# One ScalarE table behind the last head, and later places for the first unit's heads

## The chip, the cores and the metric

The kernel runs on one core of a Trainium2 chip. The core has a matrix engine (TensorE, "PE" in the profile), a vector engine (VectorE, "DVE"), an engine for functions of single elements (ScalarE, "ACT"), a general one (GpSimd, "POOL") and one that issues transfers (SyncE, "SP"); 16 DMA engines move the data. Each engine works through its own instructions in their order and waits for others by semaphores. The metric is the device time of one execution in microseconds. The time before is the median of three runs, 1692.59 us (1690.44 to 1696.43).

## What is computed

One layer of a decoder trunk (DEPTH is 1, so the convolution layer of the reference is not run), for 256 rows of 4096 numbers, all in float32:

```python
def rms_norm(x, g):
    y = x * lax.rsqrt(jnp.mean(x * x, axis=-1, keepdims=True) + 1e-6)
    return y * g

def attn_branch(xn, w_in, w_out):              # w_in 4096 x 16384, w_out 4096 x 4096
    q, k, v, g = jnp.split(xn @ w_in, 4, axis=-1)
    o = stick_breaking_attention(heads(q), heads(k), heads(v))   # 32 heads of 128
    return (o * jax.nn.silu(g)) @ w_out

# stick-breaking, strictly causal (s < t), z = q k^T / sqrt(128):
#   log_a = log_sigmoid(z) + sum of log_sigmoid(-z) over the places between s and t
#   a = exp(log_a);  out = a @ v

h = x + attn_branch(rms_norm(x, norm_attn), w_in, w_out)
return rms_norm(h, final_norm)
```

## The kernel before

**The products.** The projection by w_in is cut into 16 units (0 to 15), each with 256 columns of q, k, v and gate, which are two heads. The projection by w_out follows as four units (16 to 19). A unit runs over 16 steps s of 256 rows of the weights. All products are made in float32 precision from two rounded parts: a value is cast into a high part ("wh" of a weight, "sh" or "oh" of the activations), and the low part is the difference ("wl", "sl", "ol"). Each product is then three matmuls of 512 columns, high by high, high by low and low by high. Most units replace the eight block products of a step by seven or eight of sums and differences of blocks, and so the weights themselves need sums as well (rows that write and read "raw").

**The flow of a weight.** SyncE loads a tile into one of seven buffers "raw"; GpSimd adds a block to some of them by a transfer that accumulates; ScalarE casts wh; VectorE subtracts for wl, which frees the raw buffer for the next load; TensorE multiplies into one of seven banks of PSUM ("acc"). A weight is called by its number below: wh36 and wl36 belong to part 36.

**The heads.** When a unit's q, k, v and gate stand in SBUF ("qk_sb", "gv_sb"), `gate` applies the SiLU on ScalarE, and `heads` runs two heads one behind the other, between the next unit's products. A head (`head`) goes to and fro: TensorE turns q and k ("tr"), ScalarE copies them ("qkT"), TensorE makes the scores ("z"), ScalarE makes the softplus ("f") and its high part ("fh"), VectorE the low part ("fl"), TensorE sums along the row with a triangle of -1 ("scan", z again), ScalarE takes the exponential ("a"), TensorE multiplies by v ("o"), and VectorE multiplies by the gate. One bank "att" is shared by all of this, so a head's steps wait for each other. What the heads give is spilled to DRAM and comes back as "p" for the second projection.

**The end.** `plain_h` copies unit 16's four banks into the output rows "h" on ScalarE, once the heads' last result is spilled; unit 17 writes the same banks again. Sums with x ("xres"), squares and the gain ("grow") follow unit by unit. For the last unit, `last_h`, `block_done`, `part_done` and `finish` end the two blocks of 128 rows (t = 1 first, then t = 0): last sums out of the banks, squares, then in `finish` the inverse root as exponential of -0.5 times a logarithm on ScalarE, one step of Newton on VectorE, and `rows_out` scales the block and stores its eight tiles.

**What sets the order.** The program is written by a planner (`Plan`): it holds a model of the engines' times, and whenever an engine is free in that model, it emits the waiting piece of work with the lowest key. A key is a place on TensorE's line of products in ns; `soon(c)` is the present place plus c us, and `act` without a key takes `soon()`, that is 4 us. So a number in a key moves instructions in one engine's order, and what moves there moves the model for all others.

**Tables.** ScalarE holds one set of functions at a time. The program loads one at its start, and a later pass puts a load ahead of each function that the present set lacks (rows ACT_TABLE_LOAD).

Of the kernel before, what the change touches and what calls it, by code (L numbers as in the profile page):

```python
# [13 lines left out]
AF = mybir.ActivationFunctionType  # L14
# [5 lines left out]
P = 128  # L20
S = 256
# [26 lines left out]
TABLE = 1400  # L48
# [17 lines left out]
H_LATER = 3  # L66
GAIN_LATER = 30.0
ON_SCALAR = ((1, 3, 5), (1, 3))
AHEAD, SUMS_AHEAD = 4.0, 4.0
BLOCKS_LATER = 2  # L70
FORMS_BEHIND = 3
# [34 lines left out]
def scalar_ns(n):  # L106
    return 98 + n / 1.2
# [142 lines left out]
def kernel(  # L250
# [10 lines left out]
    nc = Plan(tc)  # L261
# [14 lines left out]
    def minus(out_, full, part):  # L276
        nc.vector.tensor_tensor(out=out_, in0=full, in1=part.bitcast(F32), op=ALU.subtract)
# [49 lines left out]
    def soon(c=4.0):  # L327
        return nc.here + 1e3 * c


    def dve(emit, n, key=None, more=0, **kw):
        n = n if isinstance(n, tuple) else (n,)
        cost = sum(vector_ns(m) for m in n) + 122 * (len(n) - 1) + more
        return nc.work("vector", cost, emit, soon() if key is None else key, **kw)

    def act(emit, n, key=None, **kw):
        n = n if isinstance(n, tuple) else (n,)
        cost = sum(scalar_ns(m) for m in n) + 100 * (len(n) - 1)
        return nc.work("scalar", cost, emit, soon() if key is None else key, **kw)
# [6 lines left out]
    def ten(emit, *n, what):  # L346
        def others():
            nonlocal since_others, words
            first_ = BEHIND.get(what, ())
            since_others, words = 0, first_ + BEHIND_OTHERS[len(first_) :]  # L350
            emit()

        return nc.work("tensor", 40 + sum(tensor_ns(m) for m in n), others, nc.here - 1e4, wait=400)
# [453 lines left out]
    st, ev = {}, {}  # L807

    def gate(u):
        yield nc.until(("gv", u))  # L810
        g = st["gv", u][:, :, 0:CW]
        n = NT * CW
        yield act(lambda: nc.scalar.activation(g, g, AF.Silu), n + TABLE)
        nc.tell(("gate", u))

    def mm3(out_, a, b, start, stop, orders):
# [8 lines left out]
    BW = 3 * P  # L825
    not_before = off.broadcast_to([P, 2, P])

    def head(u, i):
        yield nc.take("att", "gh", sooner=True)
        tr = att.tile([P, 2, S], F32, tag="att", name=f"tr{u}_{i}")  # L830

        def turn():
            for k in range(2):
                for t in range(NT):
                    c = k * CW + i * P
                    nc.tensor.transpose(tr[:, k, t * P : (t + 1) * P], st["qk", u][:, t, c : c + P], ident)

        yield ten(turn, P, P, P, P, what=("turn", i))
        if i == HG - 1:
            nc.give("one")  # L840
        qk = wp.tile([P, 2, S], F32, tag="gh", name=f"qkT{u}_{i}", bufs=ROWS)
        yield act(lambda: nc.scalar.copy(qk, tr), 2 * S)
        nc.give("att")
        yield nc.take("att", sooner=True)
        bank = att.tile([P, W], F32, tag="att", name=f"z{u}_{i}")
        z, gT = bank[:, 0:BW], bank[:, BW:W]

        def turned(to, t):
            nc.tensor.transpose(to, st["gv", u][:, t, i * P : (i + 1) * P], ident)

        def scores():
            kw = dict(stop=False, skip_group_check=True)
            nc.tensor.matmul(z[:, 0:P], qk[:, 1, P:S], qk[:, 0, P:S], start=True, **kw)
            nc.tensor.matmul(z[:, P:BW], qk[:, 1, 0:P], qk[:, 0, :], start=False, **kw)
            diagonal = z[:, 0 : 2 * P].rearrange("p (a b) -> p a b", a=2)
            nc.tensor.matmul(diagonal, ident_b, not_before, start=False, **kw)

        yield ten(scores, *FULL_P, *FULL_S, 2 * P, what=("scores", i))
        nc.give("gh")
        yield nc.take("gh", sooner=True)  # L860

        f = wp.tile([P, BW], F32, tag="gh", name=f"f{u}_{i}", bufs=ROWS)

        def soft():
            nc.scalar.activation(f, z, AF.Softplus, scale=scale)
            nc.scalar.activation(f, f, AF.Copy, scale=1.0 / scale)

        yield act(soft, (BW + TABLE, BW))
        yield nc.take("gh", "gh", sooner=True)
        fh, fl = (wp.tile([P, BW], F32R, tag="gh", name=f"f{k}{u}_{i}", bufs=ROWS) for k in "hl")  # L870
        yield act(lambda: nc.scalar.copy(fh, f), BW)
        yield dve(lambda: minus(fl, f, fh), BW)
        nc.give("gh")

        if i == 0:
            yield nc.until(("gate", u))

        def scan():
            kw = dict(start=False, skip_group_check=True)
            nc.tensor.matmul(z, neg_tri, fh, stop=False, **kw)  # L880
            nc.tensor.matmul(z, neg_tri, fl, stop=False, **kw)
            nc.tensor.matmul(z[:, 2 * P : BW], neg_one, fh[:, 0:P], stop=False, **kw)
            nc.tensor.matmul(z[:, 2 * P : BW], neg_one, fl[:, 0:P], stop=True, **kw)
            turned(gT, 0)

        yield ten(scan, BW, BW, P, P, P, what=("scan", i))
        nc.give("gh", "gh")
        gated = st["gv", u][:, :, i * P : (i + 1) * P]
        yield nc.take("gh", sooner=True)
        a = wp.tile([P, BW], F32, tag="gh", name=f"a{u}_{i}", bufs=ROWS)  # L890


        def weights_of():
            nc.scalar.activation(a, z, AF.Relu, scale=-scale)
            nc.scalar.activation(a, a, AF.Exp, scale=-1.0)

        yield act(weights_of, (BW, BW + TABLE))
        yield act(lambda: nc.scalar.copy(gated[:, 0, :], gT), P)
        nc.give("att")
        yield nc.take("att", sooner=True)  # L900
        bank2 = att.tile([P, BW], F32, tag="att", name=f"o{u}_{i}")
        o, gT2 = bank2[:, 0:S], bank2[:, S:BW]
        v = lambda t: st["gv", u][:, t, CW + i * P : CW + (i + 1) * P]

        def out_of_head():
            kw = dict(skip_group_check=True)
            nc.tensor.matmul(o, v(0), a[:, P:BW], start=True, stop=False, **kw)
            nc.tensor.matmul(o[:, P:S], v(1), a[:, 0:P], start=False, stop=True, **kw)
            turned(gT2, 1)

        yield ten(out_of_head, *FULL_P, *FULL_S, P, what=("values", i))
        nc.give("gh")
        yield act(lambda: nc.scalar.copy(gated[:, 1, :], gT2), P)
        o2 = o.rearrange("p (t b) -> p t b", t=NT)
        yield dve(lambda: nc.vector.tensor_tensor(out=gated, in0=o2, in1=gated, op=ALU.mult), S)
        nc.give("att")
# [66 lines left out]
    def make_room():  # L983
        nonlocal ep
        rooms.close()
        ep = ctx.enter_context(tc.tile_pool(name="last", bufs=1))

    def new_h(c):

        if 2 <= c < NJ - 4:  # L990
            pair = wp.tile([P, KT, W], F32, tag="wh", name=f"h{c}", bufs=HIGHS)
            for t in range(NT):
                hs[c, t] = pair[:, t, :]
            return
        if c == NJ - 4:
            raw_h = raws[:, raw_free.pop(0)]
            for t in range(NT):
                hs[c, t] = raw_h[:, t].rearrange("p k n -> p (k n)")
            return
        for t in range(NT):  # L1000
            pool, tag, bufs = (ep, f"h{c}_{t}", 1)
            if c == NJ - 3 and t == 0:
                pool, tag, bufs = wp, "gh", ROWS
            elif c >= NJ - 2:
                pool, tag = sp, "x" + "hl"[t] + str(LAST_STEPS[c - NJ + 2])
            hs[c, t] = pool.tile([P, W], F32, tag=tag, name=f"h{c}_{t}", bufs=bufs)
# [67 lines left out]

    def plain_h(u, c):
        yield nc.until(*(("spilled", v) for v in range(NB)), ("full", u, PLAIN["C11"]))
        make_room()
        for k in range(2):
            new_h(c + k)
        for k in range(2):  # L1080
            for t in range(NT):
                b = PLAIN[f"C{t + 1}{k + 1}"]
                yield nc.until(("full", u, b))
                yield act(lambda: nc.scalar.copy(hs[c + k, t], ev[u][b]), W, place_of[u + 1, 0] - 2e3)
                nc.give(f"b{b}")
        nc.tell(("C", u))
# [121 lines left out]
    def rows_out(c, t, f, key):  # L1208
        h = hs[c, t]
        if c >= NJ - 2:  # L1210
# [6 lines left out]
            )  # L1217
        elif c in ON_SCALAR[t]:
            yield act(lambda: nc.scalar.activation(h, h, AF.Copy, scale=f), W, key)
# [75 lines left out]
    for s in range(NS):  # L1295
        nc.start(blocks_of_heads(s))
    U = OUT0
    nc.start(plain_h(U, 0))
    for k, c in enumerate(range(0, NJ - 2, 2)):
        if k:  # L1300
# [44 lines left out]
```

## Time and profile before

| | us |
|---|---|
| median of three runs | 1692.59 |
| profiled execution | 1690.6 |
| its span, first to last instruction | 1688.9 |
| ScalarE busy in table loads, 84 of 1283 ns and one at the start | 109.1 |
| TensorE waits: for VectorE's wl, 5 times | 3.6 |
| TensorE waits: for ScalarE's wh, once | 0.4 |
| last matmul ends | 1671.6 |

The profile is one execution. A row of the timeline shows start and length in us, the engine, the line of the program, the operation, the tile written and the tile read, the shape, and behind it in brackets how long the engine idled before it and for whom. Nearly all instructions have line 133, a helper's; tiles tell them apart. The granted clock of TensorE was 0.996 of full speed.

### The profile page before, as it was taken

The page shows a single profiled execution, that of the slowest core. Times are in us where ns is not written, and L with a number is a line of the kernel's source. Part 1 is how long each engine was busy: PE and PEld are TensorE (multiplying, and loading weights), DVE is VectorE, ACT ScalarE, POOL GpSimd, SP SyncE. Part 2 cuts the span into 40 slices and gives each one's busy share as a digit, 9 for nine tenths or more (in the row PEclk, how much of TensorE's full clock was granted, in tenths as well). Part 3 has the DMA queues.
Part 4 walks back from the last instruction along what each step waited for, and adds up shares of the span by engine and source line. Part 5 has one row for each costly group of instructions (what it writes and reads, how often), then busy time and mean ns, then how long its engine had stood idle before and what let it go on. Part 6 is the DMA issues. An engine that isn't in the chain of part 4 may idle for free.

```text
span 1688.9 us, 24974 instructions
## 1 busy us (share of the span) xinstructions
PE 1666.1 (99%) x7731; PEld 1409.2 (83%) x7731; DVE 1611.2 (95%) x1851; ACT 1268.8 (75%) x1668; POOL 365.8 (22%) x448
## 2 busy tenths in 40 slices
PE   9999999999999999999999999999999999999995
PEld 7888888888888888888888888888888888888884
DVE  8889999999999999999999999999999978999996
ACT  8886968686868696868686868787878766656665
POOL 0022222222222222222222222222222112212110
PEclk9999999999999999999999999999999999999998
DMA  9968898988897979797979798889888977979894
GB/s 338 349 177 252 230 261 222 259 227 257 228 265 212 274 202 281 199 285 206 272 215 265 215 260 227 247 235 251 231 249 239 291 247 239 274 223 275 249 307 148
DMA packets 253174, 417.22 MB, mean 247 GB/s; under 512 B 28784, under 2 KB 77168, under 8 KB 253040
## 3 DMA queue, kind: packets, MB, share of 16 engines
q1 hardware_dynamic: 194544, 354.24, 62.9%
q0 software_dynamic: 58208, 61.11, 21.9%
q8 instruction: 60, 0.98, 0.2%
q14 instruction: 74, 0.61, 0.1%
q10 hardware_dynamic: 288, 0.28, 0.1%
HBM read 407.13 MB, written 8.39 MB: 246 GB/s over the span
## 4 chain that ended last, share of the span: by engine, by line
PE 93%; DVE 4%; issue 1%; ACT 1%; DMA 1%; SPq 0%; DVEq 0%; ACTq 0%
PE acc L133 88%; PE z L133 3%; DVE wl L133 2%; PE o L133 1%; PE tr L133 1%; DVE h L133 1%; DVE raw L133 1%; DMA raw<-in_w_out_dram 0%; ACT wh L133 0%; DMA xres<-in_x_dram 0%; ACT L133 0%; DMA raw<-in_w_in_dram 0%; DVE wh L133 0%; SPq L133 0%; ACT sq L133 0%
## 5 line engine op out<-in xcount | busy, mean ns | idle before, releaser
L133 ACT CAST wh<-raw 128x1024 fp32r<-128x1024 f32 (+1 forms) x1019 | 936.5, 966 | 326.0 <-PE acc L133 139.3
L133 DVE TENSOR_TENSOR wl<-raw,wh 128x1024 fp32r<-128x1024 f32 (+1 forms) x830 | 989.8, 1219 | 42.8 <-ACT wh L133 19.5
L133 PE MATMUL acc<-wh,sh 128*128 128x512 f32 x2048 | 766.0, 387 | 0.4 <-ACT wh L133 0.4
L133 PE MATMUL acc<-wh,sl 128*128 128x512 f32 x1883 | 721.3, 383 | 0.0
L133 PE MATMUL acc<-wl,sh 128*128 128x512 f32 x1718 | 657.7, 383 | 2.2 <-DVE wl L133 2.2
L133 POOL DMA_DIRECT2D raw<-in_w_in_dram x330 | 284.0, 945 | 1003.5 <-DMA raw<-in_w_in_dram 409.6
L133 PEld LDWEIGHTS acc<-wh,sh 128*128 128x128 f32 x2048 | 384.7, 188 | 70.9 <-ACT wh L133 0.8
L133 PEld LDWEIGHTS acc<-wh,sl 128*128 128x128 f32 x1883 | 352.8, 187 | 63.8 <-DVE sl L133 0.6
L133 PEld LDWEIGHTS acc<-wl,sh 128*128 128x128 f32 x1718 | 322.5, 188 | 58.9 <-DVE wl L133 3.6
L133 DVE TENSOR_TENSOR raw<-raw 128x512 f32<-128x512 f32 x378 | 359.9, 952 | 4.6 <-DMA raw<-in_w_out_dram 1.4
L133 PE MATMUL acc<-wh,oh 128*128 128x512 f32 x512 | 192.1, 383 | 0.0
L133 PE MATMUL acc<-wh,ol 128*128 128x512 f32 x488 | 186.5, 382 | 0.0
L133 PE MATMUL acc<-wl,oh 128*128 128x512 f32 x464 | 177.5, 383 | 1.5 <-DVE wl L133 1.4
L133 DVE TENSOR_TENSOR wh<-raw,wh 128x512 fp32r<-128x512 f32 x189 | 129.3, 684 | 1.4 <-ACT wh L133 1.4
L133 PEld LDWEIGHTS acc<-wh,oh 128*128 128x128 f32 x512 | 96.0, 187 | 17.1
L133 ACT ACT_TABLE_LOAD x84 | 107.8, 1283 | 1.5
L133 PEld LDWEIGHTS acc<-wh,ol 128*128 128x128 f32 x488 | 91.4, 187 | 16.0
L133 PEld LDWEIGHTS acc<-wl,oh 128*128 128x128 f32 x464 | 87.0, 187 | 18.1 <-DVE wl L133 2.8
L133 POOL DMA_DIRECT2D raw<-in_w_out_dram x48 | 41.8, 971 | 161.5 <-DMA raw<-in_w_out_dram 49.9
L133 POOL DMA_DIRECT2D p<-spill x28 | 17.0, 648 | 100.0 <-DVE ol L133 63.8
L133 DVE SCALAR_TENSOR_TENSOR gv_sb<-acc,scalars,gv_sb 128x512 f32<-128x512 f32 x45 | 33.5, 745 | 0.0
L133 ACT CAST oh<-p 128x512 fp32r<-128x512 f32 (+3 forms) x47 | 21.2, 471 | 13.8 <-DVE p L133 13.1
(87 smaller groups left out, 709.5 us busy)
## 6 DMA issues: line engine op xcount, KB each, us to landing
raw<-in_w_in_dram SPq DMA_DIRECT2D x1024, 256.0 KB, 4.5
raw<-in_w_out_dram SPq DMA_DIRECT2D x256, 256.0 KB, 4.4
raw<-in_w_in_dram POOLq DMA_DIRECT2D x330, 128.0 KB, 4.9
p<-spill POOLq DMA_DIRECT2D x28, 256.0 KB, 4.4
raw<-in_w_out_dram POOLq DMA_DIRECT2D x48, 128.0 KB, 5.6
xr<-in_x_dram SPq DMA_DIRECT2D x16, 256.0 KB, 5.1
spill<-gv_sb POOLq DMA_DIRECT2D x32, 128.0 KB, 4.8
xres<-in_x_dram SPq DMA_DIRECT2D x16, 256.0 KB, 5.8
```

The costliest lines, as they stand in the source:

```text
L133: return self.tc.keep_in_program_order(getattr(self.engine, name)(*args, **kw))
```

## The change

Two edits. First, `plain_h` issues a table load of its own, once the last head's result is spilled and unit 16's first bank is full, for a set that holds logarithm and exponential. Second, ScalarE's steps in `gate` and `head` get a key of their own: `soon(4.0)` as before for all units but the first, and `soon(12.0)` for unit 0, by the new number HEADS_FIRST.

```diff
+HEADS_FIRST = 12.0
@@ def gate(u):
+        act_ = lambda *w: act(*w, soon(4.0 if u else HEADS_FIRST))
-        yield act(lambda: nc.scalar.activation(g, g, AF.Silu), n + TABLE)
+        yield act_(lambda: nc.scalar.activation(g, g, AF.Silu), n + TABLE)
@@ def head(u, i):
+        act_ = lambda *w: act(*w, soon(4.0 if u else HEADS_FIRST))
-        yield act(lambda: nc.scalar.copy(qk, tr), 2 * S)
+        yield act_(lambda: nc.scalar.copy(qk, tr), 2 * S)
-        yield act(soft, (BW + TABLE, BW))
+        yield act_(soft, (BW + TABLE, BW))
-        yield act(lambda: nc.scalar.copy(fh, f), BW)
+        yield act_(lambda: nc.scalar.copy(fh, f), BW)
-        yield act(weights_of, (BW, BW + TABLE))
-        yield act(lambda: nc.scalar.copy(gated[:, 0, :], gT), P)
+        yield act_(weights_of, (BW, BW + TABLE))
+        yield act_(lambda: nc.scalar.copy(gated[:, 0, :], gT), P)
-        yield act(lambda: nc.scalar.copy(gated[:, 1, :], gT2), P)
+        yield act_(lambda: nc.scalar.copy(gated[:, 1, :], gT2), P)
@@ def plain_h(u, c):
         yield nc.until(*(("spilled", v) for v in range(NB)), ("full", u, PLAIN["C11"]))
+        yield act(lambda: nc.scalar.preload_act_table_set("natural_log_exp_and_others"), TABLE)
         make_room()
```

ScalarE's order in the first unit's first head, before, from the SiLU to the cast of weight 41:

```order
L133 ACTIVATE gv_sb0_1045<-gv_sb0_1045 128x2x256
L133 ACT_TABLE_LOAD
L133 ACTIVATE f0_0_1097<-z0_0_1083 128x384
L133 ACTIVATE f0_0_1097<-f0_0_1097 128x384
L133 CAST wh36_1015<-raw_76 128x1024
L133 CAST wh37_1016<-raw_76 128x1024
L133 CAST fh0_0_1118<-f0_0_1097 128x384
L133 CAST wh42_1131<-raw_76 128x1024
L133 CAST wh43_1150<-raw_76 128x512
L133 CAST wh40_1082<-raw_76 128x1024
L133 CAST wh41_1109<-raw_76 128x1024
```

and the same place now:

```order
L134 ACTIVATE gv_sb0_1045<-gv_sb0_1045 128x2x256
L134 CAST wh36_1015<-raw_76 128x1024
L134 CAST wh37_1016<-raw_76 128x1024
L134 ACT_TABLE_LOAD
L134 ACTIVATE f0_0_1097<-z0_0_1083 128x384
L134 ACTIVATE f0_0_1097<-f0_0_1097 128x384
L134 CAST wh42_1135<-raw_76 128x1024
L134 CAST fh0_0_1138<-f0_0_1097 128x384
L134 CAST wh40_1082<-raw_76 128x1024
L134 CAST wh43_1155<-raw_76 128x512
L134 CAST wh41_1109<-raw_76 128x1024
```

The casts of weights 36 and 37 stand ahead of the table load and the softplus now, and that of weight 42 ahead of the head's own cast. The rows of the first unit's second head move by one or two places in the same way; its table load still stands ahead of the casts of weights 52 and 53. On VectorE, the low parts of 36 and 37 come ahead of one sum of raw tiles. On TensorE, the first head's scan comes one product earlier and its values four products later.

ScalarE's order at the start of the copies of unit 16 ("oh" is the cast of a head's result "p", "h" the output rows), before:

```order
L133 CAST oh13_12971<-p13_13155 128x384
L133 COPY h0_0_13228<-acc16_1_12415 128x512
L133 CAST oh13_12971<-p13_13155 128x128
L133 COPY h0_1_13229<-acc16_6_12423 128x512
L133 CAST wh880_13238<-raw_76 128x1024
L133 CAST wh878_13185<-raw_76 128x1024
L133 COPY h1_0_13230<-acc16_7_12447 128x512
L133 CAST wh879_13209<-raw_76 128x1024
L133 COPY h1_1_13231<-acc16_3_12460 128x512
```

and now:

```order
L134 CAST oh13_12971<-p13_13155 128x384
L134 ACT_TABLE_LOAD
L134 CAST oh13_12971<-p13_13155 128x128
L134 COPY h0_0_13240<-acc16_1_12415 128x512
L134 CAST wh880_13229<-raw_76 128x1024
L134 COPY h0_1_13241<-acc16_6_12423 128x512
L134 CAST wh878_13185<-raw_76 128x1024
L134 COPY h1_0_13242<-acc16_7_12447 128x512
L134 CAST wh879_13209<-raw_76 128x1024
L134 COPY h1_1_13243<-acc16_3_12460 128x512
```

The load is new, and three of the four copies stand one place further behind among the casts. Shortly behind, on SyncE, the load of x for the second block's first sum (xres) comes behind one more weight tile.

ScalarE's order at the end ("sq" the squares, "scalars" one number per row), before, from the second block's squares:

```order
L133 ACTIVATE sq_0_0_15352,squares_of_rows<-h_0_14742 128x256
L133 ACTIVATE sq_0_256_15354,squares_of_rows<-h_0_14742 128x256
L133 ACT_TABLE_LOAD
L133 ACTIVATE scalars<-squares_of_rows,scalars 128x1
L133 ACT_TABLE_LOAD
L133 ACTIVATE scalars<-scalars 128x1
```

and now:

```order
L134 ACTIVATE sq_0_0_15353,squares_of_rows<-h_0_14743 128x256
L134 ACTIVATE sq_0_256_15355,squares_of_rows<-h_0_14743 128x256
L134 ACTIVATE scalars<-squares_of_rows,scalars 128x1
L134 ACTIVATE scalars<-scalars 128x1
```

Both loads are gone, here and in the first block: four fewer, one more near unit 16, and 82 instead of 85 in all.

## The prediction

> **What bounds the kernel now.** I read the page's busy times first, then TensorE's waits, then busy times by stage, and last the rows of the stages that the change touches.
>
> ```profile
> PE 1666.1 (99%) x7731; PEld 1409.2 (83%) x7731; DVE 1611.2 (95%) x1851; ACT 1268.8 (75%) x1668; POOL 365.8 (22%) x448
> PE 93%; DVE 4%; issue 1%; ACT 1%; DMA 1%; SPq 0%; DVEq 0%; ACTq 0%
> ```
>
> TensorE is busy for 99% of the span and holds 93% of the chain. So the time is TensorE's work, plus the little that it waits, plus what comes behind its last matmul. A change on ScalarE is worth something only in the last two. Their sizes by stage (columns: stretch and length; busy us of PE, PEld, DVE, ACT, POOL; clock, DMA share, GB/s):
>
> ```profile
> 99.63:125.20 25.57, 24.24 (x114) 19.74 (x112) 25.57 (x28) 22.37 (x30) 4.75 (x6) 1.00 0.72 202
> 170.00:1300.00 1130.00, 1130.00 (x5301) 959.82 (x5300) 1114.21 (x1188) 882.63 (x1112) 278.65 (x328) 1.00 0.86 240
> 1495.00:1568.30 73.30, 71.79 (x324) 59.91 (x322) 70.59 (x77) 44.32 (x57) 14.46 (x18) 1.00 0.85 252
> 1671.60:1688.90 17.30, 0.00 (x0) 0.00 (x0) 7.31 (x21) 7.36 (x13) 0.00 (x0) 0.65 0.65 243
> ```
>
> From 170 to 1300 TensorE has no gap at all. It lacks 1.3 us between 99.63 and 125.2, where VectorE is busy without a break (25.57 of 25.57), and 1.5 us between 1495 and 1568, where VectorE is busy for 96%. Behind the last matmul lie 17.3 us: this is the end stage.
>
> **The end: four table loads removed.** The two row blocks of 128 rows end one after the other, t = 1 first. In both, ScalarE's last square is followed by load, logarithm, load, exponential:
>
> ```profile
> 1667.52 0.19 ACT L133 ACTIVATION_READ_ACCUMULATOR sq<-h 128x1 f32 x1
> 1667.72 1.28 ACT L133 ACT_TABLE_LOAD   x1
> 1669.01 0.29 ACT L133 ACTIVATE scalars<-squares_of_rows,scalars 128x1 f32<-128x1 f32 x1
> 1669.33 1.28 ACT L133 ACT_TABLE_LOAD   x1
> 1670.62 0.20 ACT L133 ACTIVATE scalars<-scalars 128x1 f32<-128x1 f32 x1
> ...
> 1675.71 0.19 ACT L133 ACTIVATION_READ_ACCUMULATOR sq<-h 128x1 f32 x1
> 1675.92 1.28 ACT L133 ACT_TABLE_LOAD   x1
> 1677.21 0.29 ACT L133 ACTIVATE scalars<-squares_of_rows,scalars 128x1 f32<-128x1 f32 x1
> ```
>
> VectorE waits for both results:
>
> ```profile
> 1668.26 0.15 DVE L133 SCALAR_TENSOR_TENSOR scalars<-squares_of_rows,scalars 128x1 f32<-128x1 f32 x1
> 1670.86 0.22 DVE L133 SCALAR_TENSOR_TENSOR scalars<-scalars 128x1 f32<-128x1 f32 x1 [2.45 <-ACT scalars L133]
> ...
> 1674.06 0.75 DVE L133 TENSOR_TENSOR h<-acc,h 128x256 f32<-128x256 f32 x2
> ...
> 1679.05 0.22 DVE L133 SCALAR_TENSOR_TENSOR scalars<-scalars 128x1 f32<-128x1 f32 x1 [2.96 <-ACT scalars L133]
> ```
>
> What the pair takes without loads shows early in the same trace, where the first table still holds both functions:
>
> ```profile
> 84.00 0.44 ACT L133 ACTIVATE scalars<-scalars 128x2 f32<-128x2 f32 x2 [2.62 <-DVE scalars L133]
> 84.48 0.22 DVE L133 SCALAR_TENSOR_TENSOR scalars<-scalars 128x1 f32<-128x1 f32 x1 [0.32 <-ACT scalars L133]
> ```
>
> Logarithm and exponential run back to back in 0.44 us, and VectorE goes on 0.48 us after their start. So the second block's pair, starting at 1675.92 in place of the load, lets VectorE go on at 1675.92 + 0.48 + 0.09 (this logarithm takes 0.29, not about 0.20) = 1676.49, not 1679.05: **2.56 us**.
>
> For the first block the same gives 1667.72 + 0.57 = 1668.29, but VectorE is in its row of 1668.26 until 1668.41: it goes on at about 1668.43 instead of 1670.86, 2.43 us. Its work up to the last sums out of the banks, 1670.86 to 1674.06, is 3.20 us without a wait, so these sums could start at 1671.63. They also need the last matmul:
>
> ```profile
> 1671.19 0.40 PE L133 MATMUL acc<-wh,ol 128*128 128x512 f32 x1
> ```
>
> It ends at 1671.59, so the two just meet: **2.4 us**, and no larger saving in the first block could bring more. The second block's squares, and with them its pair, start 2.4 us earlier.
>
> The output must not take this back. Its transfers, by stretches (columns as above):
>
> ```profile
> 1672.70:1677.60 4.90, 0.00 (x0) 0.00 (x0) 2.43 (x7) 3.25 (x8) 0.00 (x0) 0.91 1.01 374
> 1677.60:1680.80 3.20, 0.00 (x0) 0.00 (x0) 1.64 (x6) 2.07 (x4) 0.00 (x0) 0.50 0.01 4
> 1680.80:1687.30 6.50, 0.00 (x0) 0.00 (x0) 2.21 (x4) 1.29 (x3) 0.00 (x0) 0.50 0.98 363
> ```
>
> Each block's transfers fill the DMA engines (shares 1.01 and 0.98), with 3.2 us of nothing between. The first block's move by 2.4, the second's by 2.4 + 2.56, so 3.2 - 2.56 = 0.6 us of the pause is left and the second block still starts at once. The end is worth **5.0 us**. Bounds: 2.6 (the first pair brings nothing) and 2.4 + 3.2 = 5.6 (the pause closed).
>
> The Trainium skill ("ScalarE: Activation LUTs", section "What ACT_TABLE_LOAD costs") gives 1283 ns for a load and about 1380 ns for a drain with it, 2.66 us for every switch. Here the load starts 0.01 us behind the read that ends at 1667.71, and the logarithm 0.01 us behind the load, so no drain lies on this path and the four loads are worth 1.28 each. By the page the added load below would cost ScalarE 2.66 us, the last copy there would be ready some 0.5 us too late for TensorE, and the sum would be 5.7 instead of 6.2 us.
>
> **The added load, near 1427.** It enters ScalarE ahead of the four copies that free the banks of unit 16:
>
> ```profile
> 1427.70 0.59 ACT L133 COPY h<-acc 128x512 f32<-128x512 f32 x1 [0.88 <-PE acc L133]
> 1432.56 0.59 ACT L133 COPY h<-acc 128x512 f32<-128x512 f32 x1
> ```
>
> ```profile
> 1434.73 0.38 PE L133 MATMUL acc<-wh,oh 128*128 128x512 f32 x1
> ```
>
> Most of the load fits the 0.88 us that ScalarE idles ahead of the first copy. The rest, and weight casts put ahead of copies, bring the last copy from 1432.56 to about 1433.0. The matmul that writes the same bank stands at 1434.73, 1.1 us behind that copy's end. Cost: nothing; if the cover were gone, at most the load's 1.28.
>
> SyncE's load of x for the next sum moves behind one more weight tile (two issues). Where it stood, what followed, and its use:
>
> ```profile
> 1445.24 0.33 SPq L133 DMA_DIRECT2D xres<-in_x_dram  x1
> 1446.05 1.29 SPq L133 DMA_DIRECT2D raw<-in_w_out_dram  x2
> ```
>
> ```profile
> DMA to landing us min/median/max: 4.3/5.2/5.5
> ```
>
> ```profile
> 1454.43 0.69 DVE L133 TENSOR_TENSOR h<-h,xres 128x512 f32<-128x512 f32 x1
> ```
>
> It would be issued at about 1447.3 and land by 1452.8, 1.6 us before VectorE wants it: nothing again.
>
> **The first unit's heads.** At the start of the busy stretch VectorE waits for ScalarE:
>
> ```profile
> 95.67 0.63 ACT L133 ACTIVATE gv_sb<-gv_sb 128x512 f32<-128x512 f32 x1
> 96.32 1.28 ACT L133 ACT_TABLE_LOAD   x1
> 98.56 1.98 ACT L133 CAST wh<-raw 128x1024 fp32r<-128x1024 f32 x2
> ```
>
> ```profile
> 93.80 2.55 DVE L133 TENSOR_TENSOR raw<-raw 128x512 f32<-128x512 f32 x3
> 99.62 1.23 DVE L133 TENSOR_TENSOR wl<-raw,wh 128x1024 fp32r<-128x1024 f32 x1 [3.28 <-ACT wh L133]
> ```
>
> and at its end TensorE waits for VectorE:
>
> ```profile
> 123.44 0.43 PE L133 MATMUL acc<-wh,sh 128*128 128x512 f32 x1
> 125.22 0.51 PE L133 MATMUL acc<-wl,sh 128*128 128x512 f32 x1 [1.35 <-DVE wl L133]
> ```
>
> The two starts lie 1.78 us apart where its pace is 0.22: 1.56 us lost. VectorE is not idle between 99.62 and 125.2, so its lead there is what counts. The casts of weights 36 and 37 now come before the table load. VectorE's split follows the start of its cast by 99.62 - 98.56 = 1.06, so it starts at 96.32 + 1.06 = 97.38, 2.24 us earlier. Two things take part of that back. A raw sum that lay in the old pause now stands behind weight 37: 0.64 us (three took 2.55, one of them twice as wide, so four units). And VectorE, now ahead, waits for the cast of weight 42, which still follows the head's load: ScalarE comes to it at 96.32 + 1.98 (two casts) + 1.28 (load) + 0.96 (the head's two steps, 97.60 to 98.56) = 100.54, the split to 101.6, while VectorE is there at 97.38 + 3 x 1.14 + 0.64 = 101.4 (1.14 from one wide row's start to the next: 3.49 for three in a row further below, the last of them 1.22): 0.2 us, and an estimated 0.15 in the same way for weight 46 behind the head's exponential. The order of VectorE's later steps up to weight 52, which ends TensorE's wait, is nearly unchanged, and raw buffers come back earlier, so their loads do. Lead 2.24 - 0.64 - 0.35 = **1.25 us** out of the 1.56; bounds 0 and 1.56. The head's scan stands one product (0.66 us) earlier on TensorE and its values four products later; neither adds work.
>
> **The sum**: 2.4 + 2.56 + 1.25 = 6.2 us. The profiled execution took 1690.6 us (span 1688.9 and 1.7 around it), so it would take 1684.4. The median of the three runs shown is 2.0 us above it; from there, 1692.6 - 6.2 = **1686.4 us**. A measurement here tells about 0.3%, 5.1 us, from no change: the forecast lies just beyond it.
>
> **Rivals.**
> - *The end alone* (gain 5.0, 1687.6). VectorE stays the limit up to 125 and the lead is lost, since the second head's table load still stands ahead of the cast of weight 52. For it: VectorE's 25.57 of 25.57. Against it: now that cast, the first of two, starts at 122.28, which would let VectorE split it at 123.34, and VectorE comes to it one split (1.14) behind 122.81, at 123.95; if the cast did not move at all, 0.6 us of the lead would be left. Chance 0.22; it lies at the 0.3% bound. The rows of that cast and of the three splits:
>
> ```profile
> 122.28 1.98 ACT L133 CAST wh<-raw 128x1024 fp32r<-128x1024 f32 x2
> ```
>
> ```profile
> 122.81 3.49 DVE L133 TENSOR_TENSOR wl<-raw,wh 128x1024 fp32r<-128x1024 f32 x3
> ```
>
> - *Half the end* (gain 2.6 + 1.25 = 3.9, 1688.7). The last sums do not follow the last matmul at once, or the output queue takes the first block's part. Against it: the 3.2 us pause. Chance 0.12.
> - *More* (gain 6.2 + 1.5 = 7.7, 1684.9): the shifted weights also remove the gap of 1495 to 1568. Nothing in VectorE's order there speaks for it. Chance 0.09.
> - *Slower.* The moved load of x comes too late at VectorE, which stands in order: weight splits behind it stop, their buffers stay taken, and SyncE's next loads, this unit's two other loads of x among them, come unhidden as well. Three landings of 5.5 are 16.5, less 6.2: 10.3 slower, 1702.9. It begins once the landing is over 1.6 us later than worked out above, when the weight tile put ahead has to wait for a buffer. Chance 0.03.
> - That the loads stay is excluded by the order of the program.
>
> **How the numbers follow.** The forecast's own chance is 0.54. The range takes in half the end on one side (1688.7 and 1.3 for the added load, 1690.0) and on the other the bounds 5.6 + 1.56 + 1.5 = 8.7, 1683.9, with 0.9 for runs that spread by 6 us: 1683.0 to 1690.0. Faster by over 0.3%: the forecast but for noise, the *more* case, and a third of *the end alone*: 0.62. Slower 0.03. Within 0.3%: 0.35.
>
> **What would show it.** In the profile after: no load behind the last square, and VectorE's step following about 0.6 us behind it, twice; the last sums at 1671.6 less the gain in front; a pause of some 0.6 us between the two blocks' transfers; about 12.3 us from the last matmul to the end of the span; VectorE's wait at 97 shorter, and TensorE's wait near 125 at 0.2 us. It would be wrong if a bank or a load of x stops TensorE between 1430 and 1470, or if the 1495 to 1568 gap grows.

## The result and the profile after

The changed kernel takes 1690.31 us (median of 19 runs, 1688.45 to 1691.06), the kernel before in the same series 1695.73 us (19 runs, 1689.92 to 1697.68). The ratio is 0.9974, with a 95% interval of 0.9965 to 0.9983: 4.4 us less by the means and 5.4 by the medians, about the 0.3% that the prediction calls no change. Forecast were 1686.4 us and a range of 1683.0 to 1690.0.

The runs of before are not one heap. Over the five series up to e14 there are 91: 34 lie between 1689.9 and 1693.6 (median 1691.4) and 57 between 1694.4 and 1699.8 (median 1696.8). The mean granted clock is 0.995 or 0.996 in the runs of either group, so the throttle does not make them. The profiled execution of before, 1690.6 us, is of the lower group. The changed kernel has no such second group. The rest of this document is about why.

The page of the changed kernel: busy times, and the chain's shares by engine.

```profile
PE 1671.4 (99%) x7731; PEld 1410.4 (84%) x7731; DVE 1611.8 (96%) x1851; ACT 1264.7 (75%) x1665; POOL 366.3 (22%) x448
PE 96%; DVE 1%; DMA 1%; issue 1%; ACT 0%; SPq 0%; DVEq 0%; ACTq 0%
```

TensorE is busy 5.3 us **longer** than before (1671.4 against 1666.1) with the same 7731 matmuls. The stages of the changed kernel (columns as in the prediction):

```profile
99.63:125.20 25.57, 25.17 (x121) 21.08 (x120) 25.51 (x28) 23.69 (x33) 4.19 (x6) 1.00 0.70 205
170.00:1300.00 1130.00, 1130.00 (x5278) 956.14 (x5277) 1110.23 (x1183) 879.20 (x1108) 277.73 (x328) 1.00 0.86 240
1495.00:1568.30 73.30, 72.87 (x330) 61.45 (x329) 70.25 (x77) 44.16 (x55) 13.76 (x16) 1.00 0.86 256
1674.70:1686.80 12.10, 0.00 (x0) 0.00 (x0) 5.04 (x14) 3.46 (x9) 0.00 (x0) 0.71 0.83 309
```

Read the second row against before's. Both kernels keep TensorE busy for the whole 1130 us at clock 1.00, but the changed one gets through 5278 matmuls there and the kernel before through 5301. Busy time does not show this; the count does. By the start times of numbered matmuls in the two traces (counted from 0, so that 7730 is the last), in us:

```
                          before    after
start of matmul 200        50.23    51.15
200 to 600                 87.71    86.10
600 to 6200              1196.21  1201.51
6200 to 7000              174.05   173.53
7000 to 7730              162.98   161.99
last matmul to the end     17.70    12.54
```

The sum is the 2.06 us by which the spans differ. The end brought 5.16 us (forecast 5.0) and the stretch with the first unit's heads 1.61 us (forecast 1.25); 0.52 and 0.99 us more came between 6200 and the last matmul, where no gain was forecast. Lost were 0.92 us before matmul 200, ahead of anything that the change touches, and 5.30 us where nothing was changed and nothing waits.

The end, on VectorE of the changed kernel (timeline: start, duration, tile, and in brackets the idle time before it and what ended it):

```profile
1671.61 0.22 DVE L134 SCALAR_TENSOR_TENSOR scalars<-scalars 128x1 f32<-128x1 f32 x1
...
1674.82 0.75 DVE L134 TENSOR_TENSOR h<-acc,h 128x256 f32<-128x256 f32 x2
1675.87 0.16 DVE L134 SCALAR_TENSOR_TENSOR scalars<-squares_of_rows,scalars 128x1 f32<-128x1 f32 x1 [0.30 <-ACT sq L134]
1676.41 0.16 DVE L134 SCALAR_TENSOR_TENSOR scalars<-squares_of_rows,scalars 128x1 f32<-128x1 f32 x1 [0.38 <-ACT sq L134]
1676.97 0.22 DVE L134 SCALAR_TENSOR_TENSOR scalars<-scalars 128x1 f32<-128x1 f32 x1 [0.40 <-ACT scalars L134]
```

and on ScalarE:

```profile
1676.20 0.19 ACT L134 ACTIVATION_READ_ACCUMULATOR sq<-h 128x1 f32 x1
1676.41 0.29 ACT L134 ACTIVATE scalars<-squares_of_rows,scalars 128x1 f32<-128x1 f32 x1
1676.74 0.20 ACT L134 ACTIVATE scalars<-scalars 128x1 f32<-128x1 f32 x1
```

No load stands behind the last square, and VectorE goes on 0.58 us behind its read. The last matmul starts at 1674.28 and takes 0.40, so the last sums (1674.82) follow its end by 0.14 us.

In front, VectorE and ScalarE of the changed kernel:

```profile
98.19 2.36 DVE L134 TENSOR_TENSOR wl<-raw,wh 128x1024 fp32r<-128x1024 f32 x2 [1.52 <-ACT wh L134]
```

```profile
97.12 1.98 ACT L134 CAST wh<-raw 128x1024 fp32r<-128x1024 f32 x2
99.12 1.28 ACT L134 ACT_TABLE_LOAD   x1
```

```profile
123.83 0.39 PE L134 MATMUL acc<-wh,sh 128*128 128x512 f32 x1
124.62 0.48 PE L134 MATMUL acc<-wl,sh 128*128 128x512 f32 x1 [0.40 <-DVE wl L134]
```

The two casts now stand ahead of the load. VectorE's wait is 1.52 instead of 3.28 us, and its first split starts at 98.19, which is 97.27 without the 0.92 us that this execution was late by (97.38 was worked out). And TensorE's stall near 124 is 0.79 - 0.22 = 0.57 instead of 1.56 us.

### The profile page after: what moved, and what is told of

It is laid out like the page before. It is cut to its first block, busy times and chain, and to the rows that moved or that the text cites. A ratio compares the mean times of both kernels' runs of the same rounds, so it can differ in the third digit from the quotient of the medians.

```text
span 1686.8 us, 24973 instructions
## 1 busy us (share of the span) xinstructions
PE 1671.4 (99%) x7731; PEld 1410.4 (84%) x7731; DVE 1611.8 (96%) x1851; ACT 1264.7 (75%) x1665; POOL 366.3 (22%) x448
## 4 chain that ended last, share of the span: by engine, by line
PE 96%; DVE 1%; DMA 1%; issue 1%; ACT 0%; SPq 0%; DVEq 0%; ACTq 0%
PE acc L134 91%; PE z L134 3%; PE o L134 1%; PE tr L134 1%; DVE wl L134 1%; DVE h L134 1%; DMA grow<-in_gain_out_dram 0%; DMA raw<-in_w_in_dram 0%; ACT wh L134 0%; ACT sq L134 0%; SPq L134 0%; ACT xs L134 0%; DVE raw L134 0%; DVE wh L134 0%; DVE scalars L134 0%
```

## Where the 5.3 us went: one stream, two paces

The loss is not spread evenly. In each of the units 1 to 14 there are two passages, behind the second head's scan and behind its values, of some 23 and 25 matmuls. The same matmuls of unit 1, first before, then after (timelines of TensorE):

```profile
210.25 0.38 PE L133 MATMUL acc<-wh,sh 128*128 128x512 f32 x1
210.46 0.38 PE L133 MATMUL acc<-wl,sh 128*128 128x512 f32 x1
210.69 0.38 PE L133 MATMUL acc<-wh,sl 128*128 128x512 f32 x1
...
211.34 0.38 PE L133 MATMUL acc<-wh,sl 128*128 128x512 f32 x1
```

```profile
209.56 0.40 PE L134 MATMUL acc<-wh,sh 128*128 128x512 f32 x1
209.80 0.39 PE L134 MATMUL acc<-wl,sh 128*128 128x512 f32 x1
210.02 0.39 PE L134 MATMUL acc<-wh,sl 128*128 128x512 f32 x1
...
210.71 0.40 PE L134 MATMUL acc<-wh,sl 128*128 128x512 f32 x1
```

Five steps take 1.09 us before and 1.15 us after: 218 and 230 ns a matmul (over a whole passage 223 and 230 behind the scan, 221 and 230 behind the values), no row with a wait. A passage at some 220 ns is called quick below, one at some 230 ns slow. Where a matmul in a slow passage starts more than 220 ns behind the one ahead, the rest over 220 is its surplus. It sums up to 0.23 + 0.26 us a unit, 6.86 us in all 28 passages; where a passage is taken to begin and end moves such a sum by up to 0.3 us. In before's profile the same matmuls have some surplus too, in the run-in behind each step, so that the net difference is 5.3. Every profile shows either all 28 passages slow or nearly none, unless the product order was altered (below).

What differs there is not the work but how it is entered. A matmul takes its 512 columns in one of two orders, c or e, so that a group of three matmuls (a *product*) has an order of three letters. Behind each of the heads' steps seven products have the orders ccc, ecc, eee, eee, eee, eee, cce; then eee, but for the first product of a step, which is cce or ecc by turns. From one start to the next, in ns, for the 24 matmuls behind the scan of unit 1 (from the trace's start times):

```
before  308 226 220 228 222 226 234 231 233 221 219 221 219 221 219 221 219 221 218 230 225 219 221 220
after   314 221 234 231 228 221 232 228 237 223 230 230 236 228 229 230 230 237 232 228 229 228 233 237
```

The rhythm differs from the first matmul on. Before settles at 219 and 221 by the tenth; after falls into 237, 223, 230, 230, 236, 228 and stays there.

## The experiments

### The two parts apart

`e1` keeps the table load and puts the heads back; `e2` the other way round.

```diff
 e1:
-HEADS_FIRST = 12.0
+HEADS_FIRST = 4.0
 e2:
-        yield act(lambda: nc.scalar.preload_act_table_set("natural_log_exp_and_others"), TABLE)
```

> The table load behind the last head alone; the first unit's heads as before (HEADS_FIRST 4), so TensorE's order is that of before. Theory A (TensorE has two paces for the same matmuls behind the second head's scan of each unit, 0.39 us apart per unit over 14 units, and its phase when it last waited decides which): the end is 5.1 us shorter than before (12.5 us from the last matmul to the end of the span, not 17.7), and the runs fall in two groups as those of before do, near 1685 and near 1691; a profile shows either no slow passages or all of them. Theory B (the slow pace comes from the weights' other places in the raw buffers, which the heads' edit brought): never a slow passage, and all runs 5 us below before's. Both: the wait near 123 stays at 1.5 us.

Measured: median 1690.85 us over 12 runs, ratio 0.9968 (0.9954 to 0.9981), in two groups: five at 1686.1 to 1687.9, seven at 1690.8 to 1692.2. Its profile (1691.7 us, of the upper group) has 28 slow passages and 12.54 us behind the last matmul. The slow pace thus occurs with before's order of heads and weights; theory B, that the weights' other places in the buffers make it, has fallen.

> The first unit's heads later alone; no load of its own near 1427, so the four loads of the end come back. TensorE's order is that of after. Both theories: slow passages in all 14 units (5.4 us), the wait near 123 at 0.5 to 0.6 instead of 1.5 us, the end at 17.7 us: 1693.5 to 1696.5. Theory A would also allow a run without slow passages, near 1688.5.

Measured: median 1695.57 us over 12 runs, ratio 1.0007 (0.9995 to 1.0019): one run at 1690.2, eleven at 1695.1 to 1696.5. The profile (1696.2 us) has 28 slow passages, a stall near 124 of 0.61 us and 17.73 us at the end. The heads' edit does what it was forecast to do, matmuls 200 to 600 in 86.15 instead of 87.71 us, and with it nearly every run is of the slow pace. Against before's upper group (1696.8) the eleven, median 1695.6, are 1.2 us faster, and e1's seven, median 1691.2, are 5.6 us faster. That before's upper group runs at the slow pace is inferred: no execution of it was profiled.

### Shifting the stream by a transpose or two

If the pace hung on TensorE's place against something else at its last wait, a few extra short matmuls behind that wait might change it. One (`e3`) or two (`e4`) transposes of the first unit's second head are issued twice.

```diff
             turned(gT2, 1)
+            if (u, i) == (0, 1):
+                for _ in range(1):   # e4: range(2)
+                    turned(gT2, 1)
```

> After, with one more transpose of the same data to the same place in the first unit's second head (some 0.05 us of TensorE, once, behind its last wait; all other orders as after). Theory A: it shifts TensorE's phase once, for all units behind it; if it leads into the fast pace, the slow passages vanish in all 14 units and the time is 1683 to 1684; if not, all stay and it is 1688.5 to 1691. Theory B: they stay, 1688.5 to 1691.

> As the last, with two more transposes: another shift of the same phase. Theory A: all 14 slow passages or none, 1688.5 to 1691 or 1683 to 1684. Theory B: they stay, 1688.5 to 1691.

Measured: 1690.15 us (ratio 0.998, 0.997 to 0.9991) and 1690.33 us (0.9976, 0.9965 to 0.9988), 12 runs each, none below 1688.3; 28 slow passages in both profiles. An added transpose takes 0.11 us in these traces, not 0.05. These two shifts do not change the pace.

### Other orders of columns behind the scan and the values

The slow passages behind the values end some seven matmuls behind the seventh product, whose order is cce; those behind the scan run on up to the values. So an earlier product of that order might end them sooner.

```diff
-BEHIND = {}
+BEHIND = {("scan", 1): ("ccc", "ecc", "cce"), ("values", 1): ("ccc", "ecc", "cce")}                      # e5
+BEHIND = {("scan", 1): ("cce", "ecc") * 3 + ("cce",), ("values", 1): ("cce", "ecc") * 3 + ("cce",)}      # e6
```

> The changed kernel, but the third product behind the second head's scan and behind its values is written in the order cce in place of eee, in all units; nothing else moves. In the profile of the changed kernel the slow passages (about 230 ns a matmul) run from behind these two steps of TensorE up to the seventh product, which is written cce. Theory A' (the pace is a state of TensorE's stream that an eee product only keeps and a cce product sets back): the passages shrink from 23 and 25 matmuls to about 9 each, their excess from 6.86 us to under 3.5 us, and the median falls from 1690.3 to 1686 to 1687.5. Rival (the seven products are slow for what goes on beside them, SBUF traffic or the rhythm of the other engines, and the passage's end at a cce word is chance): 28 passages of the same length, 6.86 us, median 1690.

> The changed kernel, but all seven products behind the second head's scan and values alternate cce and ecc, the orders that the first products of the other steps have. Theory A': no passage at 230 ns is kept up; what is left is the first products' own run-in, so the excess of 6.86 us falls below 3 us and the median to 1685 to 1687. Rival: 28 passages, 6.86 us, median 1690. A third outcome, that these orders in a row are themselves dearer than 220 ns (they stand only once in three steps elsewhere), would show as passages with another excess in every execution, fast ones included.

Measured: e5 1688.52 us (1685.87 to 1689.03, 4 runs; ratio 0.995, 0.9933 to 0.9967), passages of 20 and 12 matmuls, surplus 4.34 us; e6 1689.83 us (4 runs; 0.9962, 0.9947 to 0.9977), passages of 22 and 25, 5.32 us. The order does act on the pace, since nothing else was altered, but by less than expected: the values' passage halved, the scan's did not. The mixed orders of e6 run no better, and whether these orders are dearer by themselves is not told by the run.

`e7` has e6's orders in unit 8 alone.

> As e6, but in unit 8 of 17 alone. It tells whether the slow pace is handed on from unit to unit. If the state is kept over a whole unit (TensorE does not wait between 125 and 1495 us), mending unit 8 leaves units 9 to 15 fast: 14 slow passages or fewer, last matmul some 3 us earlier than the 1674 to 1677 of the slow profiles. If each unit's passages come anew from something earlier in the unit that stays as it is, only unit 8 differs: 26 slow passages, 0.4 us.

Measured: one run, 1690.44 us; 28 passages, surplus 6.78 us; only unit 8 differs. That spoke for the rival, passages that come anew in each unit. But e6's orders had not left the slow pace, so there was nothing good to hand on; e15 below decides it.

### Ending the passage behind the scan alone

```diff
-BEHIND = {}
+BEHIND = {("scan", 1): ("ccc", "ecc", "eec", "cee")}           # e9
+BEHIND = {("scan", 1): ("ccc", "ecc", "eee", "eee", "cce")}    # e10, e13; e12: the same in the kernel before
+BEHIND = {("scan", 1): ("ccc", "ecc", "cce")}                  # e11
```

> The changed kernel, with the words behind the second head's scan alone set to ccc, ecc, eec, cee; those behind the values stay ccc, ecc, eee. In the profiles a slow passage is left by two c matmuls in a row that come on the 237 ns beat of its pattern (237, 223, 230, 230, 236, 228 ...; at the exits the spacings are 234, 239, 225 and then 220). In the profile of the changed kernel matmuls 935 and 936 stand on that beat; here they are c. Theory A': the passage behind the scan ends at 938, after 10 matmuls, and the values, entered from the fast pace, stay fast as in before: excess 6.86 down to about 2 us, median 1684.5 to 1686.5. Rival (an exit is chance, the values' passage has its own cause): the values' 14 passages of 0.26 us stay, 3.6 us or more.

> As e9 with the word cce as the fifth behind the scan (matmuls 939 to 941, again on the slow beat: 230, 230, then 236): exit at 941 after 13 matmuls, values fast; excess about 2 to 2.5 us, median 1685 to 1687. Rival as in e9.

> As e5 (third word cce) behind the scan alone, the values' words as in the changed kernel. In e5 the values began fast (313, 223, 219, 220, 234, 239, 225) and fell into the slow pace at their own changed third word. Theory A': the scan's passage stays at 0.19 us, the values' 0.12 goes to about 0.04: excess 4.34 in e5 to about 3 us, median 1686 to 1687.5. Rival: the values' passage comes back at 0.26 us a unit: excess 6.3 us, median 1690.

Measured: e9 1690.31 us (10 runs, 1686.26 to 1691.81; ratio 0.9979, 0.9965 to 0.9994), 28 passages and 6.72 us: a miss, two c matmuls on that beat do not end the passage. e10 1685.87 us (4 runs, 1683.23 to 1686.38; 0.9956, 0.9939 to 0.9973): in its profile unit 1 is entered at the quick pace already; only unit 10, behind a gap (last section), is entered slow, and that passage is left at the altered product (0.13 us). e11 1686.89 us (5 runs; 0.9967, 0.995 to 0.9984): the scan's passages stay at 0.19 us each, the values' are gone, 3.15 us in all, as expected from a pace that is carried from the scan to the values. Unit 14 is the exception: it was entered quick, fell into the slow pace behind its altered product (227, 225, 222, 230, 230, 237, 233) and kept it behind the values. So the same order can begin the slow pace as well as end it.

### The change with the pace held alike

`e12` is the kernel before and `e13` the changed kernel, both with the orders of e10; `e14` is the changed kernel as it is.

> The kernel before with the fifth product behind the second head's scan in the order cce, as in e10. Theory A' (the words take most of the slow pace away; the change itself is worth the 6.2 us of the sum): a median of 1690 to 1692.5, fast in nearly all runs and some 6 us over e13. Rival (the words suit only the changed kernel's phase): the two groups of before stay, 1691 and 1696 to 1698, median 1693 or more.

> e10 again, in the same call as e12 and e14: a median of 1685 to 1686.5, 6.2 us (5 to 7.5) below e12 and 4 to 5.5 us below e14. Rival (the change itself is worth only about 4 us, and e10 was luck of four runs): less than 5 us below e12, or a second group of runs at 1689 to 1691.

> The changed kernel, unaltered: 1689.5 to 1691, all or nearly all runs in the slow pace (28 passages, 6.86 us, if its profile falls there); a fast run would take 1683 to 1685.

Measured on one chip in one series: before 1696.26 us (16 runs), e12 1691.52 (10 runs, 1690.26 to 1692.47; ratio 0.9976, 0.9967 to 0.9985), e14 1689.78 (6 runs, 1688.40 to 1691.51; 0.9967, 0.9955 to 0.998), e13 **1683.99** (5 runs, 1683.19 to 1684.89; 0.9931, 0.9919 to 0.9943). So:

- one altered product per unit takes before's upper group away (all ten runs lie in the lower group's span, whose median is 1691.4) and is worth 5.8 us to the changed kernel;
- with the pace alike, the change is worth 1691.52 - 1683.99 = 7.5 us, and in the two profiles (1690.0 and 1682.3 us of span) 1.45 us between matmuls 200 and 600, 0.0 between 600 and 6200, 1.3 behind 7000, and 5.16 at the end. The parts that were forecast thus come to 6.6 us; the 1.3 is no part of them.

From 170 to 1300 us e13 has before's count again:

```profile
170.00:1300.00 1130.00, 1130.00 (x5301) 959.97 (x5301) 1114.48 (x1188) 882.10 (x1111) 278.97 (x328) 1.00 0.86 241
```

### One product in one unit

e12's profile held a hint: only its first passage is entered slow, and it is left at the altered product. `e15` is the changed kernel with that order in unit 2 alone: two matmuls of 7731 take their columns in another order.

```diff
-BEHIND = {}
+BEHIND = {("scan of 2", 1): ("ccc", "ecc", "eee", "eee", "cce")}
...
-        yield ten(scan, BW, BW, P, P, P, what=("scan", i))
+        yield ten(scan, BW, BW, P, P, P, what=("scan of 2" if u == 2 else "scan", i))
```

> The changed kernel with one product altered: the fifth behind the second head's scan in unit 2 alone is written cce. If the pace is carried on in TensorE's stream from unit to unit (theory A'), the passages ahead of it are slow (2 or 3), unit 2's is left at the altered product, and all later ones are entered and run at 220 ns: excess of the passages 0.5 to 1 us instead of 6.86, 170 to 1300 us holds about 5299 matmuls, median 1684.3 to 1686. Rival (each unit's passages arise anew): 26 or 27 slow passages, 6.4 us or more, 5278 matmuls, median 1689.5 to 1691.

Measured: 1685.16 us (6 runs, 1684.52 to 1685.96; ratio 0.9947, 0.9929 to 0.9965), against 1690.31 and, on the same chip, 1689.78 (e14) of the changed kernel. Three slow passages are left, two in unit 1 and the first part of unit 2's (0.62 us). The altered product, at the thirteenth matmul behind the scan, in unit 2 of e15 (timeline of TensorE):

```profile
292.53 0.39 PE L134 MATMUL acc<-wh,sh 128*128 128x512 f32 x1
292.76 0.40 PE L134 MATMUL acc<-wl,sh 128*128 128x512 f32 x1
293.00 0.39 PE L134 MATMUL acc<-wh,sl 128*128 128x512 f32 x1
293.23 0.38 PE L134 MATMUL acc<-wh,sh 128*128 128x512 f32 x1
293.45 0.38 PE L134 MATMUL acc<-wl,sh 128*128 128x512 f32 x1
293.67 0.38 PE L134 MATMUL acc<-wh,sl 128*128 128x512 f32 x1
```

Spacings of 0.23 and 0.24 up to the product's third matmul, 0.23 behind it and then 0.22. What follows, by the ns from the first matmul behind the second head's scan to the next, in units 1 to 14:

```
changed kernel           314 314 313 313 313 313 313 314 314 313 313 313 313 313
e12 (before, all units)  313 308 307 307 307 308 308 307 307 307 308 308 307 307
e15 (unit 2 alone)       314 314 307 307 307 308 308 307 307 307 308 308 307 308
```

From the next unit on, every scan is entered at 307 or 308, as in the profile of before, though those units have the old order. The pace is handed on through the 389 matmuls from one unit's scan to the next. The rival, that each unit's passages arise anew, would have left 26 slow passages. From 290 to 1300 us, e15 gets through 4733 matmuls and the changed kernel through 4713:

```profile
290.00:1300.00 1010.00, 1010.00 (x4733) 857.90 (x4732) 995.21 (x1059) 785.42 (x987) 249.81 (x294) 1.00 0.86 241
```

```profile
290.00:1300.00 1010.00, 1010.00 (x4713) 854.52 (x4712) 991.82 (x1054) 782.04 (x984) 248.75 (x294) 1.00 0.86 240
```

### One pair of loads back

`e8` loads the joint table behind the first row block's exponential instead of near 1427, so that the first block has its two loads again and the second has none.

```diff
-        yield act(lambda: nc.scalar.preload_act_table_set("natural_log_exp_and_others"), TABLE)
...
             nc.scalar.activation(r, r, AF.Exp, scale=-0.5)
+            if t == 1:
+                nc.scalar.preload_act_table_set("natural_log_exp_and_others")
```

> The changed kernel, but the joint table is loaded behind the first row block's logarithm and exponential instead of near 1427 us: the first block (t = 1) has its two loads back, the second has none. It measures the two terms of the end apart. The prediction's terms: from the last matmul to the end of the span 12.54 + 2.4 = 15.0 us (before 17.7, changed 12.54). Rival (the first pair counts for less, since the last sums wait for the last matmul anyway, half the end): 12.6 to 13.5 us. The load itself, 1.28 us on ScalarE between the blocks, should lie beside VectorE's work and cost nothing.

Measured: one run, 1693.63 us; 15.42 us from the last matmul to the end, 2.88 more than in the changed kernel. VectorE of e8 there:

```profile
1676.17 0.22 DVE L134 SCALAR_TENSOR_TENSOR scalars<-scalars 128x1 f32<-128x1 f32 x1 [2.45 <-ACT scalars L134]
...
1678.20 0.16 DVE L134 TENSOR_REDUCE scalars<-squares_of_rows 128x1 f32<-128x7 f32 x1 [0.46 <-ACT sq L134]
...
1679.92 0.75 DVE L134 TENSOR_TENSOR h<-acc,h 128x256 f32<-128x256 f32 x2
```

0.46 us of it is a new wait: the moved load itself holds up the second block's square, which was expected to cost nothing. The first pair is worth some 2.88 - 0.46 = 2.42 us. The rival, that it counts for little, fell.

## Why the prediction was wrong

Point by point:

- **The end, 5.0 us: right.** It measured 5.16, and 2.42 for the first pair where 2.4 was forecast. The last sums meet the last matmul (0.14 us behind it), VectorE follows the last square by 0.58 us, and 12.54 us lie behind the last matmul where 12.3 were expected. The pause in the output's transfers shrank to about 0.6 us, as worked out:

```profile
DMA  9999999999999508999999999999999999400000
```

(the changed kernel's DMA share from 1674 to 1686.8 us in 40 slices of 0.32 us: low in two and a half of them).

- **The added load, nothing: right.** ScalarE idles 3.09 and 1.16 us ahead of the two casts in front of it, and TensorE has no gap between 1425 and 1495 us. ScalarE there:

```profile
1432.31 1.28 ACT L134 ACT_TABLE_LOAD   x1
1433.60 0.30 ACT L134 CAST oh<-p 128x128 fp32r<-128x128 f32 x1
1433.81 0.58 ACT L134 COPY h<-acc 128x512 f32<-128x512 f32 x1
```

The cast starts 0.01 us behind the load. By the Trainium skill ("ScalarE: Activation LUTs", section "What ACT_TABLE_LOAD costs") a drain of about 1380 ns goes with each switch; these rows and the end's 5.16 us for four loads show none. The prediction's price by that figure, 0.5 us, does not follow from its own rows: 1433.0 + 1.38 + 0.59 is 1434.97, 0.24 us behind the matmul at 1434.73.

- **The load of x, nothing: right.** It lands at 1458.26 and VectorE takes it at 1459.09 without a wait, with 0.83 us to spare where 1.6 was worked out; the slower case did not come about.
- **The first unit's heads, 1.25 us: near in sum (1.61), not in its parts.** The stall near 124 fell by 0.99, with 0.57 left where 1.56 - 1.25 = 0.31 was worked out. Some 0.5 us more came ahead of it (matmul 520 starts 0.51 us nearer to matmul 200), where before's profile has two passages of the slow pace at 105 to 116 us and the changed one has none. The prediction had not counted those.
- **Beyond the rivals**: the late stretch (*more*) was no steady gain; TensorE's gaps between 1495 and 1575 came to 0.6 us in the first profile of the changed kernel, 1.0 in its second (e14), 1.4 in e13 and 2.6 in e15, which are alike there, and to 2.0 in that of before.
- **The step that failed** is the last: "The profiled execution took 1690.6 us ... so it would take 1684.4". It takes TensorE's 1130 us without a gap as a fixed length: of the head's two moved steps it says "neither adds work", and puts the cost of the long stretch at nothing. The execution that the savings were taken from was of the quicker of two paces, and the changed kernel nearly always gets the slower one: 5.3 us, as much as the whole end. Where both are of the same pace the forecast holds: 7.5 us from e12 to e13 (6.6 in the parts forecast), and 6.5 us from before's upper group (1696.8) to the changed kernel (1690.3), where 6.2 was forecast. The other base, 1692.59, was the middle one of three runs, two of the lower group and one of the upper. Counted from medians, 3.1 of the 3.9 us by which the forecast is off are this base (1695.73 by 19 runs) and 0.8 the gain (5.4 for 6.2). That the medians differ by nearly the forecast gain is luck: most of before's runs happened to be of the slow pace too.

Shown is that the same matmuls run at two paces, that the order of columns can end the slow one, and that a pace is mostly handed on from unit to unit. Why the change picks the slow one is not shown. The runs go with the heads' place: with before's heads and a stall of about 1.6 us near 124 (before and e1) 34 of 91 and 5 of 12 runs came out quick, with the later heads and a stall of about 0.6 us (the changed kernel, e2 to e4) 1 of 61. But that stall does not set the pace in a way that TensorE's rhythm shows. In the profiles of before and of the changed kernel (as in those of e1 and e14) the matmuls from 554 to 782, at 128 to 178 us and thus behind the stall, start at spacings that agree to 2 ns; the first that differs is the turn of q and k in unit 1's first head (234 ns before, 228 after). What the state consists of, within TensorE or between it and the engines beside it, stays open. e3, e4 and e9 show that two simple guesses, a shift by a transpose and an exit on a certain beat, are not enough.

## What to carry to other kernels

Where an engine is busy without a gap, compare not its busy time but how many instructions it completes in the same stretch, and check on several runs which group the profiled execution belongs to before a saving is added to it. A gain of a few microseconds in front can come with a slower stream far behind it, in work that was not changed. Where a long stream runs at one of two paces, one altered instruction order at one place may be worth more than the whole change: e13, the change with one product per unit altered, is the fastest version here, 0.9931 of before.

## What was not expected of the hardware

- The same fp32r matmuls of 512 columns, at granted clock 1.00 and without a wait, start every 220 or every 230 ns, and the state lasts: 389 matmuls with transposes, scores, scan and values between do not wipe it out. The Trainium skill ("TensorE: Matmul & The Clock Gate", section "Back-to-back issue gap") gives for one matmul by itself N / 2.4 + 2.5 ns, 216 for 512 columns, and for a sustained stream of weight loads and matmuls about 131. The quick pace is near the first, no stretch here is near the second, and the slow pace is in neither.
- It can be flipped by the order in which two matmuls take their columns (e15, 5.1 us of 1690). It also flipped behind short gaps: in e11 the unit behind a gap of 0.34 us at 1260 was entered quick (307) after thirteen slow ones (313 or 314), and in e10 the one behind a gap of 0.26 us at 876 was entered slow (313) after nine quick ones. A gap is neither enough nor needed: two of 0.10 us at 595 in e10 changed nothing, and in e13 unit 2 was entered slow (313) behind a quick unit 1 (310) with no gap between them.
